# Splitting the left operands of the down product where they are made

## Chip, cores and metric

The kernel runs on one core of a Trainium2 chip. The metric is the device time of one execution in microseconds (us). All data are float32. TensorE (PE) multiplies, VectorE (DVE) and GpSimd (POOL) do elementwise work, ScalarE (ACT) does copies and activation functions, and the queue of SyncE (SP) issues the DMAs.

## What is computed

One block of an encoder for 1024 tokens of width 1024: a SwiGLU layer of half weight, a combined attention of two kinds, a second SwiGLU layer, with an RMSNorm before and after each.

```python
def _rmsnorm(x, g):
    r = lax.rsqrt(jnp.mean(x * x, axis=-1, keepdims=True) + EPS)
    return x * r * g

def _swiglu(x, w_gate, w_up, w_down):            # D_FF = 2816 = 22 * 128
    return (jax.nn.silu(x @ w_gate) * (x @ w_up)) @ w_down

f = _swiglu(_rmsnorm(x, ffn1_pre_g), ffn1_w_gate, ffn1_w_up, ffn1_w_down)
x = x + 0.5 * _rmsnorm(f, ffn1_post_g)
h = _rmsnorm(x, mix_pre_g)
qkv = h @ w_qkv
...
x = x + _rmsnorm(heads @ w_out, mix_post_g)
f = _swiglu(_rmsnorm(x, ffn2_pre_g), ffn2_w_gate, ffn2_w_up, ffn2_w_down)
x = x + 0.5 * _rmsnorm(f, ffn2_post_g)
```

## The kernel before

Every float32 operand of a product is split into two parts of a shorter float type (HI, and LO, the rest), and a product runs as three passes (HI HI, HI LO, LO HI). The function `split` makes the parts: an ACT copy for HI (L118), then a subtraction on DVE or POOL for LO (L119).

Both SwiGLU layers are objects of the class `Ffn`, with the same code. Their products are done in 2 x 2 blocks by a scheme that needs seven products in place of eight (P1 to P7). The gate and up weights are worked through in 22 column blocks i of 128. Blocks 1 to 21 run as items ("G", i, product), each of 12 matmuls of 128 x 512, in the order of `ORDER`: P1, P6, P2, P7, P5, P4, P3 (`LAST` for block 21). P2 adds to the PSUM bank on which P1 stood, after P1 has been copied out to the tile U (`gate_up`, L416). The sums U and C (tiles U2, U3, C21) are formed by DVE; `glu` takes silu on ACT (L449) and multiplies on DVE (L450). Its results are the four left operands of the down product for each pair j of blocks: tiles h of 128 x 512. `feed` prepares weights up to five tiles ahead of their use: for gate/up it splits the loaded weights (tile wgu from rawgu), and POOL forms their sums in place (L215, L216, L225, L227).

Pairs j = 0 to 10 of blocks make up the inner dimension of the down product, with seven products k each; 77 items ("D", k, j), 12 matmuls each. `GROUPS` takes pairs 0 to 4 first, then 5 to 10. After the odd block of a pair, `keep` stores the seven left operands of the pair to DRAM (hd): three as they are, four after an add on DVE, which are queued in `late` and emitted one for each item that follows (`add_late`). `load_left` loads them back (tile h, pool of `HBUFS` = 10), in the order of use, which begins with product 1 of pairs 0 to 4; `AHEAD` = 4 loads come early. `prepare_down` splits both operands of an item, left (h) and right (blocks b11 to b22 of the down weights).

What sets the order is the order of emission; on each engine instructions run in the program's order, and each waits for what it reads or overwrites. SP's queue holds loads and stores in one order as well.

In the first layer, `run` takes `jobs`: the post norms of rows 4 to 7 and parts of the next layer's norm (`stat1`, `post1`, `mix1`, `turn1`) are emitted between the last items of the down phase; what is left stands between the layer and the qkv projection.

Of the kernel before, what the change touches and what calls it, by code (L numbers as in the profile page):

```python
# [36 lines left out]
def tile_macaron_block(ctx, tc, x, f1_pre, f1_post, f1_g, f1_u, f1_d, mix_pre, mix_post, w_qkv,  # L37
# [83 lines left out]
    class Ffn:  # L121
# [6 lines left out]

        ORDER = ("P1", "P6", "P2", "P7", "P5", "P4", "P3")
# [8 lines left out]
        AHEAD = 4  # L138

        def __init__(self, wg, wu, wd, tag, far):  # L140
# [8 lines left out]
            for it in self.items:  # L149
                self.tiles += [it] if it[0] == "G" else [it + (z,) for z in range(2)]  # L150
            self.wanted = [d[1:] for d in downs]
            self.hd = {}
            for key in self.wanted:
                self.hd[key] = dram.tile([128, 512], F32, name=f"hd{tag}" + "_".join(str(z) for z in key))
            self.made = self.used = 0
            self.dw = {}
            self.late, self.late2 = [], []
# [43 lines left out]
        def feed(self):  # L201

            while self.made < len(self.tiles) and self.made - self.used < self.WBUFS:
                it = self.tiles[self.made]
                self.made += 1
                {"G": self.prepare, "D": self.prepare_down}[it[0]](*it[1:])
# [32 lines left out]
        def load_left(self, n):  # L239

            for _ in range(n):
                if self.wanted:
                    key = self.wanted.pop(0)
                    self.A[key] = self.dn.tile([128, 512], F32, name="h")
                    SP.dma_start(self.A[key], self.hd[key])

        def prepare_down(self, k, j, part):

            sub, add, tt = OP.subtract, OP.add, DVE.tensor_tensor
            if part == 0:  # L250
                self.load_left(1)
                self.split_w((j, k, 0), self.A.pop((k, j)), DVE)
                return
# [6 lines left out]
            self.split_w((j, k, 1), (b11, b21, b11, b12, b12, b11, b22)[k], DVE)  # L260
# [73 lines left out]
        def keep(self, j):  # L334

            a11, a21, a12, a22 = [self.H[2 * j + c][b] for c in range(2) for b in range(2)]
            for k, t in ((0, a11), (1, a12), (4, a22)):
                SP.dma_start(self.hd[k, j], t)
            S = {"a11": a11, "a12": a12, "a22": a22, "s1": a21}

            def made(k, o, p, q, op):
                if o not in S:
                    S[o] = self.dn.tile([128, 512], F32, name="h")
                DVE.tensor_tensor(S[o], S[p], S[q], op=op)
                SP.dma_start(self.hd[k, j], S[o])

            for z in ((5, "s1", "s1", "a22", OP.add), (2, "s2", "s1", "a11", OP.subtract),
                      (3, "s3", "a22", "s2", OP.subtract), (6, "s4", "a12", "s2", OP.subtract)):
                self.late.append(lambda z=z: made(*z))

        def down(self, k, js, y, ps, psd, row=None):
# [6 lines left out]
            for i in range(4):  # L358
# [6 lines left out]
                for j in js:  # L365
                    A, B = [self.W[j, k, z].rearrange("p a k f -> p a (k f)") for z in range(2)]
                    for n, (a, b) in enumerate(PASSES):
                        PE.matmul(p, A[:, a, 128 * i:128 * i + 128], B[:, b, :],  # L368
# [10 lines left out]
                elif k == 2:  # L379
                    tt(U[i], U[i], p, op=add)  # L380
                    if g:
                        self.late += [lambda v=v, i=i: tt(v, v, U[i], op=add) for v in (y11, y10)]
                        self.late2.append(lambda v=y01, i=i: tt(v, v, U[i], op=add))
# [18 lines left out]
        def gate_up(self, i, prod, ps, y, psd):  # L402
# [40 lines left out]
            if n == 6 and i % 2 == 1:  # L443
                self.keep(i // 2)
            if n == 6 and i == NF - 1:
                self.U = [U(name).rearrange("p t f -> p (t f)") for name in ("U2", "U2", "C21", "U3")]
# [5 lines left out]
        def run(self, ps, y, psd, jobs, row):  # L452
# [4 lines left out]
            for n, it in enumerate(self.items):  # L457
                if n == at:
                    self.late += self.late2
                    self.add_late(len(self.late) - len(self.late2))  # L460
# [3 lines left out]
                if n < at - 18 or n >= at - 6 or n >= at - 12 and n % 2 == 0:  # L464
# [7 lines left out]
                else:  # L472
                    self.down(it[1], it[2:], y, ps, psd)
                    self.used += 2
# [83 lines left out]
    def post_early(T, g):  # L558
# [6 lines left out]
        DVE.tensor_tensor(yh, yh, g[:, 0:512], op=OP.mult)  # L565
# [87 lines left out]
    def early1():  # L653
        for T in range(4):
            post_early(T, E1["g"])
# [549 lines left out]
```

## Time and profile before

| what | us |
|---|---|
| median of three runs | 2038.09 (2037.31 to 2041.84) |
| profiled execution | 2038.71 |
| its span in the trace | 2036.9 |
| gate/up, first layer, about | 60 to 472 |
| down, first layer, about | 472 to 695 |
| gate/up, second layer, about | 1392 to 1802 |
| down, second layer, about | 1802 to 2025 |

The span is the time from the first to the last instruction in the trace; the profiled execution takes 1.8 us more than it. A duration in a row is that of one instruction or of a run of equal ones. "Idle before" is the time that the engine stood still ahead of an instruction, with the instruction of another engine that ended it. A matmul's end is modelled, so that two may overlap in a row.

### The profile page before, as it was taken

What the parts mean: (1) busy time and instruction counts of PE and PEld (TensorE: products, weight loads), DVE (VectorE), ACT (ScalarE), POOL (GpSimd) and SP (SyncE); (2) the same over time, 40 slices, a digit from 0 to 9 for tenths busy, and PEclk for the clock granted to TensorE, in tenths of its full rate; (3) what the DMA queues carried; (4) which work ended last, traced back from release to release, by engine and by line L of the source; (5) the groups of instructions that cost most, each with busy time, mean ns of one, the idle gap of its engine ahead of it and who ended that gap; (6) DMA issues with size and microseconds to landing.
All of it is one profiled execution on the core that took longest, in us unless ns stands there. A gap on an engine that the chain in (4) does not pass through costs nothing.

```text
span 2036.9 us, 30471 instructions
## 1 busy us (share of the span) xinstructions
PE 1976.9 (97%) x10704; PEld 1675.1 (82%) x10704; DVE 1351.0 (66%) x2435; ACT 1030.5 (51%) x1977; POOL 840.7 (41%) x768
## 2 busy tenths in 40 slices
PE   7999999999999899999999999999999999999996
PEld 6777777778878699998999998887777777788785
DVE  7645554557878838756989888356545455577787
ACT  5433333334445734547999999234333333344444
POOL 4566656560000002124777887315565666600000
PEclk9999999999999899999999999999999999999998
DMA  5232332428534542232050743322223232375343
GB/s 150 74 102 95 113 103 79 130 82 274 182 109 144 183 131 78 78 93 59 1 140 13 205 133 93 104 78 73 94 88 121 86 104 93 109 268 176 120 130 138
DMA packets 212441, 235.62 MB, mean 116 GB/s; under 512 B 22209, under 2 KB 148161, under 8 KB 212161
## 3 DMA queue, kind: packets, MB, share of 16 engines
q1 hardware_dynamic: 212288, 233.69, 36.7%
q8 instruction: 84, 1.38, 0.3%
q14 instruction: 69, 0.56, 0.1%
HBM read 166.01 MB, written 67.63 MB: 115 GB/s over the span
## 4 chain that ended last, share of the span: by engine, by line
PE 70%; POOL 11%; ACT 6%; DVE 5%; issue 4%; DMA 3%; SPq 0%; DVEq 0%; ACTq 0%; POOLq 0%
PE pq L608 10%; PE pd L368 8%; PE pa L294 8%; PE pc L294 6%; PE pd L294 5%; PE pt L935 5%; POOL wgu L119 5%; PE pz L1073 4%; PE pb L294 3%; PE pa L368 3%; ACT wgu L118 3%; PE po L959 3%; PE pb L368 3%; PE pc L368 3%; PE sp L845 3%
## 5 line engine op out<-in xcount | busy, mean ns | idle before, releaser
L119 POOL TENSOR_TENSOR wgu<-rawgu,wgu 128x512 fp32r<-128x512 f32 x216 | 312.9, 1457 | 359.5 <-ACT wgu L118 333.4
L118 ACT ACTIVATE wgu<-rawgu 128x512 fp32r<-128x512 f32 x302 | 181.7, 628 | 377.6 <-POOL rawgu L227 189.6
L294 PE MATMUL pa<-actT,wgu 128*128 128x512 f32 (+1 forms) x1080 | 268.2, 395 | 7.9 <-ACT U L416 7.9
L294 PEld LDWEIGHTS pa<-actT,wgu 128*128 128x128 f32 x1080 | 197.1, 189 | 63.5 <-ACT U L416 20.1
L368 PE MATMUL pd<-wgu 128*128 128x512 f32 x948 | 236.3, 393 | 7.5 <-DVE wgu L119 6.9
L368 PEld LDWEIGHTS pd<-wgu 128*128 128x128 f32 x948 | 178.3, 189 | 49.2 <-DVE wgu L119 10.6
L608 PE MATMUL pq<-wq,actT 128*128 128x256 f32 x1728 | 217.4, 283 | 0.6 <-DVE actT L109 0.6
L608 PEld LDWEIGHTS pq<-wq,actT 128*128 128x128 f32 x1728 | 208.4, 189 | 1.4 <-DVE actT L109 0.9
L118 ACT ACTIVATE wgu<-b 128x512 fp32r<-128x512 f32 x154 | 97.2, 631 | 218.9 <-PE pd L368 209.6
L73 POOL TENSOR_SCALAR gpost<-gpost 128x1024 f32<-128x1024 f32 x2 | 2.6, 1294 | 387.5 <-DVE wgu L119 194.5
L838 POOL TENSOR_SCALAR P<-P,il 128x1024 f32<-128x1024 f32 (+1 forms) x128 | 130.5, 1020 | 66.7 <-DVE il L837 62.7
L119 DVE TENSOR_TENSOR wgu<-b,wgu 128x512 fp32r<-128x512 f32 x154 | 106.1, 689 | 76.5 <-ACT wgu L118 76.4
L450 DVE TENSOR_TENSOR h<-h,C 64x512 f32<-64x512 f32 x42 | 49.6, 1182 | 160.8 <-ACT h L449 160.8
L939 DVE TENSOR_TENSOR PT<-pt,PT 128x512 fp32r<-128x512 f32 (+1 forms) x256 | 146.0, 611 | 2.0 <-ACT PT L938 2.0
L294 PE MATMUL pc<-actT,wgu 128*128 128x512 f32 x552 | 136.5, 395 | 0.0
L294 PE MATMUL pd<-actT,wgu 128*128 128x512 f32 x552 | 136.0, 395 | 0.0
L938 ACT ACTIVATE PT<-pt 128x512 fp32r<-128x512 f32 (+1 forms) x256 | 125.2, 544 | 12.3 <-PE pt L935 8.8
L935 PE MATMUL pt<-identr,P 128*128 128x128 f32 x896 | 124.9, 274 | 2.0 <-ACT vst L773 1.0
L294 PEld LDWEIGHTS pd<-actT,wgu 128*128 128x128 f32 x552 | 103.4, 187 | 25.3
L294 PEld LDWEIGHTS pc<-actT,wgu 128*128 128x128 f32 x552 | 103.4, 188 | 25.3 <-DVE actT L109 0.4
L294 PE MATMUL pb<-tx,wgu 128*128 128x512 f32 x504 | 122.9, 392 | 0.0
L294 PE MATMUL pc<-tx,wgu 128*128 128x512 f32 x504 | 122.4, 392 | 0.0
(204 smaller groups left out, 3978.6 us busy)
## 6 DMA issues: line engine op xcount, KB each, us to landing
hd<-h SPq DMA_DIRECT2D x154, 256.0 KB, 2.8
h<-hd SPq DMA_DIRECT2D x154, 256.0 KB, 2.9
rawgu<-in_ffn_w_gate_dram SPq DMA_DIRECT2D x88, 256.0 KB, 3.0
rawgu<-in_ffn_w_up_dram SPq DMA_DIRECT2D x88, 256.0 KB, 3.5
b<-in_ffn_w_down_dram SPq DMA_DIRECT2D x88, 256.0 KB, 3.6
bkT<-kd SPq DMA_DIRECT2D x32, 320.0 KB, 7.6
rawq<-in_w_qkv_dram SPq DMA_DIRECT2D x16, 512.0 KB, 4.9
bV<-vd SPq DMA_DIRECT2D x8, 640.0 KB, 3.9
```

The lines of the kernel that those rows point to most:

```text
L118: ACT.activation(hi, raw, AF.Copy)
L119: return eng.tensor_tensor(lo, raw, f32(hi), op=OP.subtract).ins
L294: PE.matmul(p[:, c0:c1, :], w[:, a, k, :], self.rhs(name, b, k)[:, c0:c1, :], start=(first and n == 0), stop=(n == 11), skip_group_check=True)
L368: PE.matmul(p, A[:, a, 128 * i:128 * i + 128], B[:, b, :], start=(first and start and j == js[0] and n == 0), stop=(end and j == js[-1] an ...
L608: PE.matmul(p, actT[:, a, k, T, :], WQ[j][:, b, k, :], start=(n == 0), stop=(n == 23))
L838: POOL.tensor_scalar(P[:, 0:w], P[:, 0:w], il, 1.0, op0=OP.mult, op1=OP.mult)
L845: PE.matmul(sp[:, 512 * half:512 * half + 512], col(qT[:, h, :], T), kT[:, a, 512 * half:512 * half + 512], start=(a == 0), stop=(a == 1))
L935: PE.transpose(out=p[:, j, :], in_=col(P, b0 + j), identity=ident)
L938: ACT.activation(hv, p[:, 0:n, :], AF.Copy)
L939: DVE.tensor_tensor(lv, p[:, 0:n, :], f32(hv), op=OP.subtract)
L959: PE.matmul(o, V[:, k, :], pt[:, a, k, :], start=(n == 0), stop=(n == 15))
L1073: PE.matmul(p[:, 512 * dh:512 * dh + 512], actT[:, a, c, T, :], WO[c][:, b, 512 * dh:512 * dh + 512], start=(n == 0), stop=(n == 23))
```

## The change

The left operands are split in gate/up, when they are made. `keep` queues seven jobs for a pair. Each does its add (if it has one), splits the operand by an ACT copy and a DVE subtraction into a row of y (which is free at that time; y holds the layer's rows before and after), and stores both halves with one DMA of 512 KB. `load_left` loads two halves of 256 KB, and `prepare_down` splits the right operand alone, so that five prepared tiles are five items. `AHEAD` is 2; at the last gate/up item seven late jobs and three loads are emitted, then one load for each item. The norms of rows 6 and 7 move into `run`.

```diff
-        AHEAD = 4
+        AHEAD = 2
...
-                self.tiles += [it] if it[0] == "G" else [it + (z,) for z in range(2)]
+                self.tiles.append(it)
...
-                self.hd[key] = dram.tile([128, 512], F32, name=f"hd{tag}" + "_".join(str(z) for z in key))
+                self.hd[key] = dram.tile([128, 1024], F32, name=f"hd{tag}" + "_".join(str(z) for z in key))
...
+                if it[0] == "D" and not self.dw:
+                    break
...
-                    self.A[key] = self.dn.tile([128, 512], F32, name="h")
-                    SP.dma_start(self.A[key], self.hd[key])
-
-        def prepare_down(self, k, j, part):
+                    self.A[key] = [self.dn.tile([128, 512], FR, name="h") for _ in range(2)]
+                    for z, t in enumerate(self.A[key]):
+                        SP.dma_start(f32(t), self.hd[key][:, 512 * z:512 * z + 512])
+
+        def prepare_down(self, k, j):
...
-            if part == 0:
-                self.load_left(1)
-                self.split_w((j, k, 0), self.A.pop((k, j)), DVE)
-                return
...
-        def keep(self, j):
+        def keep(self, j, y):
 
             a11, a21, a12, a22 = [self.H[2 * j + c][b] for c in range(2) for b in range(2)]
-            for k, t in ((0, a11), (1, a12), (4, a22)):
-                SP.dma_start(self.hd[k, j], t)
-            S = {"a11": a11, "a12": a12, "a22": a22, "s1": a21}
-
-            def made(k, o, p, q, op):
-                if o not in S:
-                    S[o] = self.dn.tile([128, 512], F32, name="h")
-                DVE.tensor_tensor(S[o], S[p], S[q], op=op)
-                SP.dma_start(self.hd[k, j], S[o])
-
-            for z in ((5, "s1", "s1", "a22", OP.add), (2, "s2", "s1", "a11", OP.subtract),
-                      (3, "s3", "a22", "s2", OP.subtract), (6, "s4", "a12", "s2", OP.subtract)):
-                self.late.append(lambda z=z: made(*z))
+            S = {0: a11, 1: a12, 4: a22, 5: a21, 3: y[:, 7, 0:512], 6: y[:, 7, 512:1024]}
+
+            def made(n, k, p=None, q=None, op=None):
+                if op:
+                    if k == 2:
+                        S[k] = self.dn.tile([128, 512], F32, name="h")
+                    DVE.tensor_tensor(S[k], S[p], S[q], op=op)
+                st = y[:, n, :]
+                hi, lo = [st[:, 512 * z:512 * z + 512].bitcast(FR) for z in range(2)]
+                split(hi, lo, S[k], DVE)
+                SP.dma_start(self.hd[k, j], st)
+
+            for n, z in enumerate(((0,), (1,), (4,), (5, 5, 4, OP.add), (2, 5, 0, OP.subtract),
+                                   (3, 4, 2, OP.subtract), (6, 1, 2, OP.subtract))):
+                self.late.append(lambda n=n, z=z: made(n, *z))
...
-                self.keep(i // 2)
+                self.keep(i // 2, y)
             if n == 6 and i == NF - 1:
+                self.add_late(7)
+                self.load_left(self.HBUFS // 2 - self.AHEAD)
...
-                if n < at - 18 or n >= at - 6 or n >= at - 12 and n % 2 == 0:
+                if not at - 18 <= n < at - 12:
                     self.add_late(1)
...
-                    self.used += 2
+                    self.used += 1
+                    self.load_left(1)
...
-            post_scale(Ts, post_rstd(Ts), E1["g"], [E1["xr", T] for T in Ts], lambda T: x1d[T], 512)
+            post_scale(Ts, post_rstd(Ts), E1["g"], [E1["xr", T] for T in Ts], lambda T: x1d[T])
...
-           {0: [begin1, lambda: stat1((4, 5)), lambda: post1(4)], 1: [lambda: post1(5)], 3: [lambda: mix1((4, 5))],
-            5: [early1], 6: [first_q], 7: [lambda: stat1((6, 7)), lambda: post1(6)], 8: [lambda: post1(7)],
-            9: [lambda: turn1(4), lambda: turn1(5)]}, row1)
+           {0: [begin1, lambda: stat1((4, 5)), lambda: post1(4)], 1: [lambda: post1(5)], 2: [lambda: stat1((6, 7))],
+            3: [lambda: mix1((4, 5)), lambda: post1(6)], 4: [lambda: post1(7)], 5: [early1], 6: [first_q],
+            7: [lambda: mix1((6, 7))], 8: [lambda: turn1(4)], 9: [lambda: turn1(5), lambda: turn1(6)]}, row1)
...
-    mix1((6, 7))
+    turn1(7)
     mix1((0, 1))
-    turn1(6)
     first(0, 4)
-    turn1(7)
     first(0, 5)
```

The first place is ACT's queue around the end of a block of gate/up. Before, the silu of C is followed at once by the copy L416 of the next block's P1 (pa) to U:

```order
L449 ACTIVATE C21_2192<-U3_2251 64x512
L118 ACTIVATE wgu_2295<-rawgu_2091 128x2x4x64
L449 ACTIVATE h_2229<-C21_2192 64x512
L118 ACTIVATE wgu_2316<-rawgu_2091 128x2x4x64
L449 ACTIVATE C21_2192<-U2_2191 64x512
L416 ACTIVATE U2_2334<-pa_2321 128x512
L118 ACTIVATE wgu_2340<-rawgu_2194 128x2x4x64
```

After the change, at the end of the odd block of a pair (L452 is the silu, L417 the copy of P1; y<-h is the ACT half of a left operand's split):

```order
L452 ACTIVATE C21_2554<-U3_2613 64x512
L118 ACTIVATE wgu_2657<-rawgu_2439 128x2x4x64
L452 ACTIVATE h_2591<-C21_2554 64x512
L118 ACTIVATE y_154<-h_2591 128x512
L118 ACTIVATE wgu_2675<-rawgu_2439 128x2x4x64
L452 ACTIVATE C21_2554<-U2_2553 64x512
L118 ACTIVATE y_154<-h_2633 128x512
L417 ACTIVATE U2_2694<-pa_2681 128x512
```

Two copies y<-h have moved in, one behind the silu of h and one ahead of the copy L417. At the end of an even block the first of them stands there alone.

The second place is DVE's queue at the same end of a block, after the change (L453 is the product in `glu`, L434 the update of U by P3; y<-h,y is the subtraction of a split):

```order
L431 TENSOR_TENSOR C_2997<-U_2996,pc 128x512
L453 TENSOR_TENSOR h<-h,C_2997 64x512
L119 TENSOR_TENSOR y<-h,y 128x512
L434 TENSOR_TENSOR U_2996<-U_2996,pd 128x512
L119 TENSOR_TENSOR wgu<-rawgu,wgu 128x2x4x64
L453 TENSOR_TENSOR h<-C_2997,U_2996 64x512
```

The subtraction stands between the product in `glu` and the update of U; before, the update followed the product directly.

The third place is SP's queue at the start of the first layer's down phase. In hd11_2 the first 1 is the layer, the second the product, and 2 is the pair. Before, the loads of the first items are followed by weight blocks:

```order
L245 DMA h_3703<-hd11_1_75 128x512
L245 DMA h_3705<-hd11_2_76 128x512
L245 DMA h_3707<-hd11_3_77 128x512
L245 DMA h_3709<-hd11_4_78 128x512
L237 DMA b21_3725<-in_ffn1_w_down_dram 128x512
L237 DMA b21_3727<-in_ffn1_w_down_dram 128x512
L237 DMA b21_3729<-in_ffn1_w_down_dram 128x512
L237 DMA b21_3731<-in_ffn1_w_down_dram 128x512
L237 DMA b22_3733<-in_ffn1_w_down_dram 128x512
L245 DMA h_3758<-hd10_0_79 128x512
L237 DMA b22_3778<-in_ffn1_w_down_dram 128x512
L338 DMA hd11_10_144<-h_3755 128x512
```

After the change, the stores of pair 10's left operands (L347) stand among the loads:

```order
L347 DMA hd11_10_144<-y_154 128x1024
L347 DMA hd14_10_132<-y_154 128x1024
L249 DMA h_3959<-hd11_2_76 128x512
L347 DMA hd15_10_138<-y_154 128x1024
L347 DMA hd12_10_120<-y_154 128x1024
L347 DMA hd13_10_126<-y_154 128x1024
L347 DMA hd16_10_150<-y_154 128x1024
L249 DMA h_3960<-hd11_2_76 128x512
L249 DMA h_3963<-hd11_3_77 128x512
L249 DMA h_3964<-hd11_3_77 128x512
L249 DMA h_3967<-hd11_4_78 128x512
```

The reload of hd11_2 has moved behind two stores of pair 10, and its second half behind all of them but the first operand's.

## Rows read from the trace of the kernel before

**Rows 1.** Page, part 1: busy us (share of the span) and instructions of each engine.

```profile
PE 1976.9 (97%) x10704; PEld 1675.1 (82%) x10704; DVE 1351.0 (66%) x2435; ACT 1030.5 (51%) x1977; POOL 840.7 (41%) x768
```

**Rows 2.** Waits of PE over the run: us in total, times, longest us.

```profile
PE pa L294 <- ACT U L416: 7.9, 18, 2.2
```

**Rows 3.** Chain of waits, window 395 to 425: start us, us, what.

```profile
414.67 0.63 ACT h L449
...
416.60 0.70 DVE U L433
...
417.38 0.63 ACT C L449
...
418.04 0.61 ACT U L416
...
421.75 2.75 PE pc L294 x12
```

**Rows 4.** Timeline of PE, three starts of P2: start us, us, instruction, idle before.

```profile
379.24 0.73 PE L294 MATMUL pa<-actT,wgu 128*128 128x512 f32 x2 [0.23 <-ACT U L416]
...
398.79 0.68 PE L294 MATMUL pa<-actT,wgu 128*128 128x512 f32 x2
...
418.69 0.73 PE L294 MATMUL pa<-actT,wgu 128*128 128x512 f32 x2 [0.23 <-ACT U L416]
```

**Rows 5.** Timeline of ACT, 396 to 418.

```profile
398.09 0.60 ACT L416 ACTIVATE U<-pa 128x512 f32<-128x512 f32 x1
...
401.85 0.59 ACT L449 ACTIVATE h<-pa 64x512 f32<-64x512 f32 x1 [2.12 <-PE pa L294]
...
407.53 1.16 ACT L118 ACTIVATE wgu<-rawgu 128x512 fp32r<-128x512 f32 x2 [4.43 <-POOL rawgu L216]
```

**Rows 6.** Groups of instructions by form, window 100 to 440.

```profile
L118 ACT ACTIVATE wgu<-rawgu 128x512 fp32r<-128x512 f32 x122 | 73.1, 628 | 151.9 <-POOL rawgu L227 79.4 <-POOL rawgu L216 71.7
...
L344 DVE TENSOR_TENSOR h<-h 128x512 f32<-128x512 f32 x34 | 32.2, 947 | 0.9
...
L450 DVE TENSOR_TENSOR h<-C,U 64x512 f32<-64x512 f32 x35 | 24.4, 698 | 22.3 <-ACT C L449 22.3
L450 DVE TENSOR_TENSOR h<-h,C 64x512 f32<-64x512 f32 x18 | 22.2, 1235 | 76.6 <-ACT h L449 76.6
...
L433 DVE TENSOR_TENSOR U<-U,pd 128x512 f32<-128x512 f32 x18 | 12.4, 687 | 0.6
```

**Rows 7.** Timeline of DVE, end of gate/up of the first FFN.

```profile
473.37 0.68 DVE L433 TENSOR_TENSOR U<-U,pd 128x512 f32<-128x512 f32 x1
473.96 0.69 DVE L119 TENSOR_TENSOR wgu<-h,wgu 128x512 fp32r<-128x512 f32 x1
```

**Rows 8.** DMA issues: out<-in, count, KB each, median us to landing.

```profile
h<-hd SPq DMA_DIRECT2D x154, 256.0 KB, 2.9
```

**Rows 9.** Timeline of PE, start of the down phase and waits with ends.

```profile
471.64 0.63 PE L368 MATMUL pa<-wgu 128*128 128x512 f32 x2
...
665.14 3.70 PE L368 MATMUL pd<-wgu 128*128 128x512 f32 x9 [2.92 <-DVE wgu L119]
...
690.03 0.73 PE L368 MATMUL pa<-wgu 128*128 128x512 f32 x2 [2.12 <-DVE wgu L119]
...
704.61 0.69 PE L107 MATMUL pd<-identr,y 128*128 128x128 f32 x2 [4.08 <-ACT y L647]
```

**Rows 10.** Windows of core 0: busy us (count) by engine, granted clock, DMA share, GB/s.

```profile
472.00:695.00 223.00, 215.28 (x943) 175.47 (x942) 181.99 (x304) 113.17 (x207) 1.06 (x1) 0.99 0.52 167
695.00:729.00 34.00, 29.33 (x216) 28.50 (x216) 22.70 (x62) 25.68 (x53) 0.00 (x0) 0.85 0.59 185
666.00:668.00 2.00, 2.00 (x6) 1.55 (x5) 2.00 (x9) 1.69 (x5) 0.00 (x0) 0.50 0.87 260
...
690.00:692.00 2.00, 1.97 (x9) 1.63 (x10) 2.00 (x4) 0.00 (x0) 0.00 (x0) 1.00 0.92 248
704.00:713.00 9.00, 7.80 (x34) 7.18 (x35) 5.77 (x12) 9.00 (x17) 0.00 (x0) 0.50 0.80 269
```

More of the change, by code (lines that the diff above doesn't have):

```diff
@@ L153, in __init__ @@
             for key in self.wanted:
-                self.hd[key] = dram.tile([128, 512], F32, name=f"hd{tag}" + "_".join(str(z) for z in key))
+                self.hd[key] = dram.tile([128, 1024], F32, name=f"hd{tag}" + "_".join(str(z) for z in key))
             self.made = self.used = 0
             self.dw = {}
-            self.late, self.late2 = [], []
+            self.late = []
         def open_raw(self):
@@ L259, in prepare_down @@
             b11, b12, b21, b22 = [self.B[j, name] for name in self.BLOCKS]
-            self.split_w((j, k, 1), (b11, b21, b11, b12, b12, b11, b22)[k], DVE)
+            self.split_w((j, k), (b11, b21, b11, b12, b12, b11, b22)[k], DVE)
             def diff(j):
@@ L365, in down @@
                 for j in js:
-                    A, B = [self.W[j, k, z].rearrange("p a k f -> p a (k f)") for z in range(2)]
+                    A, B = self.A[k, j], self.W[j, k].rearrange("p a k f -> p a (k f)")
                     for n, (a, b) in enumerate(PASSES):
-                        PE.matmul(p, A[:, a, 128 * i:128 * i + 128], B[:, b, :],
+                        PE.matmul(p, A[a][:, 128 * i:128 * i + 128], B[:, b, :],
                                   start=(first and start and j == js[0] and n == 0),
@@ L381, in down @@
                     if g:
-                        self.late += [lambda v=v, i=i: tt(v, v, U[i], op=add) for v in (y11, y10)]
-                        self.late2.append(lambda v=y01, i=i: tt(v, v, U[i], op=add))
+                        self.late += [lambda v=v, i=i: tt(v, v, U[i], op=add) for v in (y11, y10, y01)]
                 elif g:
@@ L458, in run @@
                 if n == at:
-                    self.late += self.late2
-                    self.add_late(len(self.late) - len(self.late2))
+                    self.add_late(len(self.late))
                     for name in ("b12", "b11"):
@@ L556, in tile_macaron_block, with post_early @@
     SS = {}
-    def post_early(T, g):
+    def post_early(T, g=None):
         if T % 2 == 0:
@@ L564, in post_early @@
                        accum_out=SS[T // 2][:, 0, T % 2:T % 2 + 1])
-        DVE.tensor_tensor(yh, yh, g[:, 0:512], op=OP.mult)
+        if g is not None:
+            DVE.tensor_tensor(yh, yh, g[:, 0:512], op=OP.mult)
     def post_late(T):
@@ L654, in early1 @@
         for T in range(4):
-            post_early(T, E1["g"])
+            post_early(T)
     def turn1(T):
```

## The prediction

> **What bounds the kernel now.** I read the busy table first: TensorE (PE) is busy 97% of the span, VectorE (DVE) 66%, ScalarE (ACT) 51% [rows 1]. So a change can gain only where PE waits, and can lose wherever something on another engine gets late. The list of PE's waits is short. Most of it lies in the down phases, behind DVE's splits, and one wait ahead of the qkv projection. Then there are 18 waits for the copy of product P1 out of bank a (L416), 7.9 us together [rows 2]. They are in the gate/up phases, are small, and are what matters here, so I read the chain of waits over one block of gate/up [rows 3]. It is a closed loop. P2 accumulates on the bank that P1 used, so it cannot start before L416 has copied P1 out. From P2's matmuls (398.79 [rows 4]) the chain goes to the silu of h (401.85, after an idle 2.12 that PE ends [rows 5]), which stands ahead of a weight split in ACT's queue. POOL's split and its sums for the next block (L215, L216) follow, then ACT's next copies (407.53, after an idle 4.43 that POOL ends [rows 5]), POOL's next work, and then the tail in [rows 3]: the silu of h (414.67), DVE's U update L433 (416.60), the silu of C (417.38), the U copy L416 (418.04), and P2 of the next block (418.69 [rows 4]). P2 starts at 379.24, 398.79 and 418.69, at two of them after an idle 0.23 [rows 4]. At 398.79 the copy (start 398.09, 0.60) had ended 0.1 us earlier [rows 5]. So there is at most 0.1 us to spare. One item is 2.75 us of matmuls [rows 3], and a pair of blocks takes 39.45 us. Whatever is put into the loop's serial part lengthens the block.
>
> **What the change puts there.** Per pair of blocks seven splits (an ACT copy into y, a DVE subtraction) move from the down phase into gate/up. Their places are seen in the two lists of ACT and the one of DVE. After an even block, the copy y<-h stands behind the silu of h, and DVE's subtraction of it stands ahead of the U update. The copy needs the h that DVE's L453 has just finished, so copy and subtraction run one after the other before the U update may start: 0.63 + 0.69 us by the nearest rows (the ACT copy of 128x512, 628 ns; DVE's 128x512 ops that have POOL idle beside them, 687 ns) [rows 6]: **1.32**. After an odd block the same stands there, and a second copy stands between the silu of C and the U copy. It splits the h that L453 has to finish after that silu (0.69), then the copy itself takes 0.63: another 1.32, **2.64** in all. A pair of blocks: 3.96.
>
> The other four splits of a pair stand right behind the U copy, while P2 runs, and behind the first weight split after P2. There ACT is idle 2.12 us before 401.85 and 4.43 before 407.53 [rows 5], so their copies cost nothing directly. Without that idle each would cost its 0.63.
>
> **Contention.** DVE's h<-h,C takes 1235 ns with a POOL op beside it, the same shape h<-C,U takes 698 with POOL idle; the add L344 takes 947 on average [rows 6]. All seven new subtractions read two SBUF operands, and some five of them lie beside the POOL part of the loop. If each stretches POOL by as much as L344 is stretched (0.26 over 687), a pair costs 1.3 more, with rounding up to 1.6. The least is 0. The stretch of before that has such adds beside POOL (398.79 to 418.69, 19.90) is 0.35 longer than its neighbour (19.55) [rows 4]; I take 0.4, near that row. The Trainium skill's page "GPSIMD Engine Reference", section "8. Key points", says that GpSimd shares its SBUF interfaces with VectorE and contends with VectorE instructions that have two SBUF inputs, and so speaks against the change. The 1235 beside 698 agrees.
>
> **Sum of gate/up.** Pairs run 0 to 10; the last one's late work falls into the down phase, and the first blocks are still filling, so nine full pairs (the 18 waits of [rows 2] are nine for each FFN). 9 x 3.96 = 35.6, with contention 9 x 4.36 = 39.2; times two FFNs, since both run the same code: 71 to 78. At the high bound (1.6 of contention, ten pairs) it is 111. I take **+78**. PE should then wait 0.23 + 1.32 + 0.4, some 1.9 us, before the P2 that follows an even block, and 2.5 (2.64 less the 0.1) before the one that follows an odd block.
>
> **Start of the down phase.** SP's list shows the reload of the third item (hd11_2: product 1, pair 2) behind two stores of the last late splits, and its second half behind the last store. Those stores wait for DVE. From the U update (473.37 in before) DVE has 20 operations in order up to the last subtraction. Such ops start 0.59 apart [rows 7], with their waits some 0.61, so the last ends near 485.6, the store and the second half are issued at 486.3, and a reload takes 2.9 from issue to landing [rows 8], so it lands at 489 to 490.5 with two halves and stores in the queue. The first half (after 9 or 10 operations, 479.5) lands at 482 to 483. PE begins the down phase at 471.64 [rows 9] and wants the item at 471.64 + 2 x 2.75 = 477.1. It waits 5 to 6 us for the first half, works 8 of 12 matmuls (1.8), and waits 4.5 to 6 for the other: 9.5 to 11.5. After idle stretches of 2.92 and 4.08 [rows 9] the granted clock stands at 0.50, the lower level, for some us (666 to 668, 704 to 713 [rows 10]). In before, idle time plus this is the price; I add 2 for it. **13.5 per FFN, 27 in all** (bounds 18 and 32).
>
> **What comes back.** A down item no longer splits its left operand: 0.63 on ACT and 0.69 on DVE less, 77 times per FFN. DVE is busy 182 of 223 us there [rows 10], and is what PE waits for. The look-ahead of the right operands also doubles in items (five tiles are five items, before two and a half). FFN1's down phase takes 223.0 with PE busy 215.3: 7.7 us idle, and some 2 to 3 us of half clock after 665.14. FFN2 runs the same code. I take 9 and 10 of some 10 in each. Ahead of qkv, 695 to 729 has 4.7 us idle and a half clock over 704 to 713 [rows 10], after the 4.08 us wait for L647 [rows 9]. The norms of rows 6 and 7 (the L647 that PE waits for) now run inside the down phase, where ACT and DVE have the room that the splits left. I take 5 (bounds 2 and 6). post_scale over whole rows adds about 0.6 for each of the four rows at the end, beside qkv matmuls, where PE does not wait; uncovered it would be 2.4 in all. **-24.** Stores and loads of hd double, from 256 KB to 512 KB an item. At a DMA share of 0.52 in the down phase [rows 10] the second reload fits, and its stores are gone from there.
>
> **Sum.** 2038.71 (the profiled run, 0.6 above the median of the three; its span is 2036.9) + 78 + 27 - 24 = 2119.7, so **2120**. The likeliest case alone reaches from 2098 (no contention 71, start 18, gains 30) to 2160 (gate/up 111, start 32, gains 22).
>
> **Rivals.**
> The clock falls too. A wait of 2.5 us before every second P2 lies between 2.12 (690.03), after which the clock stays at 1.00, and 2.92 (665.14), after which it is 0.50 [rows 9, 10]. The lower level covers the 2 us of that row, from 666, and what lies on both sides of it; I take 3.8 us from 665.14 on, in which half the rate costs 1.9, all of it in P2, which is part of the loop. 18 such waits are +34: 2154. For it: 2.5 is in the open middle, and a POOL op stretched by 0.4 makes it 2.9. Against: PE is busy without a break for the 16 us before. Chance 0.24.
> The splits are hidden. If the queues run on so that copy and subtraction fit into idle time (between ACT's silu of h, 414.67 to 415.30, and its silu of C at 417.38 lies only one copy of 0.63 [rows 3, 6]), gate/up costs nothing and the sum is 2038.7 + 27 - 24 = 2041, within 0.2%. Against: that idle time is itself the wait on L433, which comes later by the same amount. Chance 0.10.
> Faster. The splits are hidden and the start wait is short as well: if the adds and subtractions on DVE before the last store take under 12 us, or the reloads are taken around them, each FFN's start costs 9 or less, below its 12 of gain: 2038.7 + 18 - 26 = 2031. It needs the DVE string at the start of the down phase to be the only place that decides, and that string cut to half of its 20 operations. The freed 0.69 of DVE per item speaks for it. Chance 0.10.
>
> **Numbers.** Likeliest 0.56. A difference of 0.2% (4 us) is about what a measurement of this kernel tells from no change. Faster 0.10, the same 0.05, slower 0.85: the likeliest case and the clock rival are slower, 0.80, and the hidden-splits case (2041, bounds 2028 to 2049) gives 0.05 to the same and 0.05 to slower, and the last rival its 0.10 to faster. For 8 in 10 the range covers the likeliest case and the clock rival but for their ends: 2075 to 2165.
>
> **What would show it.** In the changed profile: some 18 waits on the U copy (now L417) in each FFN, of 1.9 and 2.5 us in turn, and stretches of 22.2 and 21.6 us in place of 19.55 and 19.90; waits at the third item of each down phase of 4 to 6 us, twice; no waits on DVE's wgu later in it; no 4 us ahead of qkv. It is wrong if gate/up keeps its 39.45 us a pair, or if the waits before P2 are longer than these insertions because a POOL op is stretched more than 0.4.

## The result and the profile after

The changed kernel takes 2143.1 us (median of four; 2140.8 to 2144.7) beside 2038.6 of the kernel before: a ratio of 1.051 (95% interval 1.049 to 1.053), 104.5 us slower. The profiled span is 2139.0, 102.1 more than before. The forecast was 2120, in a range of 2075 to 2165.

The two traces were laid side by side by PE's first instruction of each stage:

| stretch, by PE's timeline | before | after | difference |
|---|---|---|---|
| start to the first down item | 471.6 | 523.8 | +52.2 |
| first down phase, to the first qkv matmul | 223.1 | 226.9 | +3.8 |
| qkv, to the first transpose behind it (L771, now L773) | 144.8 | 136.7 | -8.0 |
| attention and out projection, to the second gate/up | 515.5 | 517.4 | +1.9 |
| second gate/up, to the first down item | 447.2 | 497.5 | +50.3 |
| second down phase, to the end of its matmuls | 222.2 | 224.6 | +2.4 |

So 102.5 us are lost in the two gate/up phases, and the rest comes to nothing. The busy table of the changed kernel, which answers to [rows 1]:

```profile
PE 1987.4 (93%) x10704; PEld 1677.0 (78%) x10704; DVE 1438.1 (67%) x2431; ACT 1035.4 (48%) x1977; POOL 854.3 (40%) x768
```

PE is busy 93% in place of 97%. Its waits, in the list that answers to [rows 2], name the places:

```profile
PE pa L294 <- ACT U L417: 47.9, 22, 2.3
PE pc L294 <- DVE U L422: 39.7, 20, 2.0
PE pa L370 <- DMA h<-hd: 19.1, 4, 6.0
PE pd L294 <- DVE U L425: 9.4, 18, 0.6
```

The 18 waits for the copy of P1 were 7.9 us; now there are 22, and they take 47.9. New are two groups that the prediction does not have, for the U updates L422 and L425 on DVE: 49.1 us. PE's timeline over one pair of blocks shows them in order (P2, P4, P3, the next P2, and the P2 after that; compare [rows 4]):

```profile
398.78 3.07 PE L294 MATMUL pa<-actT,wgu 128*128 128x512 f32 x12 [2.29 <-ACT U L417]
...
409.31 3.05 PE L294 MATMUL pc<-actT,wgu 128*128 128x512 f32 x12 [1.98 <-DVE U L422]
412.90 3.04 PE L294 MATMUL pd<-actT,wgu 128*128 128x512 f32 x12 [0.54 <-DVE U L425]
...
421.34 2.98 PE L294 MATMUL pa<-actT,wgu 128*128 128x512 f32 x12
...
443.26 2.13 PE L294 MATMUL pa<-actT,wgu 128*128 128x512 f32 x8 [2.29 <-ACT U L417]
```

A pair takes 443.26 - 398.78 = 44.48 us in place of 39.45: the even block 22.56 (19.90 before), the odd one 21.92 (19.55 before). One wait of 2.29 stands at the odd block's end; 1.98 and 0.54 stand inside the even block; the P2 that follows the even block waits for nothing. The chain of waits into the odd block's end is the one that the prediction drew, with the two copies y<-h in it (compare [rows 3]):

```profile
437.40 1.24 DVE h L453
438.66 0.63 ACT y L118
...
439.94 0.69 DVE U L434
440.71 0.64 ACT C L452
441.37 0.70 DVE h L453
442.09 0.63 ACT y L118
442.72 0.48 ACT U L417
```

From the product in `glu` (437.40) to P2 (443.26) are 5.86 us. Before, the product started at 415.33, and to P2 at 418.69 were 3.36:

```profile
415.33 1.24 DVE L450 TENSOR_TENSOR h<-h,C 64x512 f32<-64x512 f32 x1 [4.47 <-ACT h L449]
```

That is 2.50 more now. The other place is seen in DVE's timeline inside the even block, ahead of L422:

```profile
403.72 1.33 DVE L343 TENSOR_TENSOR y<-h 128x512 f32<-128x512 f32 x1
404.98 1.78 DVE L119 TENSOR_TENSOR y<-h,y 128x512 fp32r<-128x512 f32 x1
406.68 1.76 DVE L343 TENSOR_TENSOR y<-h 128x512 f32<-128x512 f32 x1
408.48 0.69 DVE L422 TENSOR_TENSOR U<-U,pc 128x512 f32<-128x512 f32 x1
```

and in that of POOL at the same time:

```profile
404.47 1.74 POOL L218 TENSOR_TENSOR rawgu<-rawgu 128x512 f32<-128x512 f32 x1
406.29 1.61 POOL L219 TENSOR_TENSOR rawgu<-rawgu 128x512 f32<-128x512 f32 x1
```

Adds and subtractions that take 0.69 alone take 1.33 to 1.78 here, one after the other, and L422 stands behind them. It reads bank c, and P4 cannot start on that bank before L422 has ended (409.17). POOL's sums take 1.74 and 1.61 in place of 1.29.

PE's timeline at the start of the first down phase (compare [rows 9]) and two windows of it (compare [rows 10]):

```profile
523.83 0.86 PE L370 MATMUL pa<-wgu,h 128*128 128x512 f32 x3
...
535.51 1.19 PE L370 MATMUL pa<-wgu,h 128*128 128x512 f32 x2 [6.00 <-DMA h<-hd]
...
542.15 0.80 PE L370 MATMUL pa<-wgu,h 128*128 128x512 f32 x1 [2.89 <-DMA h<-hd]
```

```profile
523.83:750.00 226.17, 217.28 (x950) 178.66 (x949) 143.43 (x240) 85.13 (x151) 1.60 (x1) 0.97 0.78 267
535.00:539.00 4.00, 3.49 (x8) 2.48 (x8) 3.97 (x8) 0.70 (x2) 0.00 (x0) 0.50 1.02 405
```

The third item waits for its two halves, 6.00 and 2.89 us, and the clock then stands at 0.50.

### The profile page after: what moved, and what is told of

Same layout as the page of the kernel before. It is cut to its first block, busy times and chain, and to the rows that moved or that the text cites. A ratio compares the mean times of both kernels' runs of the same rounds, so it can differ in the third digit from the quotient of the medians.

```text
span 2139.0 us, 30720 instructions
## 1 busy us (share of the span) xinstructions
PE 1987.4 (93%) x10704; PEld 1677.0 (78%) x10704; DVE 1438.1 (67%) x2431; ACT 1035.4 (48%) x1977; POOL 854.3 (40%) x768
## 3 DMA queue, kind: packets, MB, share of 16 engines
q8 instruction: 85, 1.39, 0.3%
## 4 chain that ended last, share of the span: by engine, by line
PE 60%; DVE 15%; POOL 9%; ACT 7%; issue 5%; DMA 3%; SPq 0%; DVEq 0%; POOLq 0%; ACTq 0%
PE pd L370 9%; PE pq L612 9%; PE pa L294 6%; PE pt L937 5%; POOL wgu L119 4%; PE pz L1075 4%; PE pd L294 3%; PE pb L294 3%; ACT wgu L118 3%; PE pa L370 3%; PE pb L370 3%; PE po L961 3%; PE pc L370 3%; DVE y L119 3%; DVE y L343 3%
## 5 line engine op out<-in xcount | busy, mean ns | idle before, releaser
L119 POOL TENSOR_TENSOR wgu<-rawgu,wgu 128x512 fp32r<-128x512 f32 x216 | 304.9, 1420 | 449.9 <-ACT wgu L118 435.4
L118 ACT ACTIVATE wgu<-rawgu 128x512 fp32r<-128x512 f32 x302 | 186.4, 625 | 271.9 <-POOL rawgu L230 127.6
L294 PE MATMUL pa<-actT,wgu 128*128 128x512 f32 (+1 forms) x1080 | 269.1, 397 | 48.8 <-ACT U L417 47.9
L370 PE MATMUL pd<-wgu,h 128*128 128x512 f32 x948 | 232.6, 391 | 0.0
L370 PEld LDWEIGHTS pd<-wgu,h 128*128 128x128 f32 x948 | 178.8, 189 | 37.8 <-DVE U L434 0.5
L294 PE MATMUL pc<-actT,wgu 128*128 128x512 f32 x552 | 141.0, 405 | 39.7 <-DVE U L422 39.7
L119 DVE TENSOR_TENSOR y<-h,y 128x512 fp32r<-128x512 f32 x110 | 111.2, 1012 | 44.6 <-ACT y L118 44.6
L294 PEld LDWEIGHTS pd<-actT,wgu 128*128 128x128 f32 x552 | 102.1, 188 | 40.3 <-issue 16.7
```

What stands on the lines that cost most here:

```text
L118: ACT.activation(hi, raw, AF.Copy)
L119: return eng.tensor_tensor(lo, raw, f32(hi), op=OP.subtract).ins
L294: PE.matmul(p[:, c0:c1, :], w[:, a, k, :], self.rhs(name, b, k)[:, c0:c1, :], start=(first and n == 0), stop=(n == 11), skip_group_check=True)
L370: PE.matmul(p, A[a][:, 128 * i:128 * i + 128], B[:, b, :], start=(first and start and j == js[0] and n == 0), stop=(end and j == js[-1] an ...
```

## The experiments

All times are medians of four to ten runs, but for five kernels that ran once: no subtractions, half of each store, held splits, one SBUF input, and POOL for the last pair alone. The kernel before took 2038.6 to 2041.0 beside them.

**The norms alone.** The kernel before with the later part of the diff: the jobs of `f1.run`, `post_early` without the gain, whole rows in `post_scale`.

> The kernel before with the reordered norms of the first layer alone; the left operands are split in the down phase as before. If the norms are what empties the wait ahead of the qkv projection (the changed kernel gained 8.0 us from the first qkv matmul to the first transpose behind it): that stretch is 6 to 8 us shorter here too, the 4.08 us wait for L647 is gone, and the whole is 4 to 8 us faster than before (about 2032). Rival: the norms only fit because the down phase has lost 77 splits; here DVE and ACT are still full, the down phase grows by what the transition loses, and the whole is within 3 us of before.

2031.6 us, ratio 0.9955 (0.9941 to 0.9968). From the first qkv matmul to the first transpose behind it the trace takes 135.9 us (144.8 before), and of the wait of 4.08 us on the norm's ACT copy 0.8 is left. The first down phase, to the first qkv matmul, takes 224.0 (223.1 before), so it does not take up what the transition loses. The reordered norms gain 9 us by themselves, a little more than expected, without the room that the splits leave, and the rival falls. This is the fastest kernel of the study.

**No subtractions.** In `made`:

```diff
-                split(hi, lo, S[k], DVE)
-                SP.dma_start(self.hd[k, j], st)
+                ACT.activation(hi, S[k], AF.Copy)
+                SP.dma_start(self.hd[k, j][:, 0:512], st[:, 0:512])
```

> The changed kernel without the seven DVE subtractions of a pair in gate/up; the ACT copies and the adds remain. Left out is the LO part of the left operands (the HI half is stored, half as much, and loaded twice). Theory of the prediction (insertions at the ends of blocks alone, pair 3.96): an odd end keeps two copies and the wait for the product in glu, some 1.9 us before P2, an even end 0.5; a pair is near 42. What the trace of the changed kernel suggests (DVE's string of adds and subtractions ahead of the U updates L422 and L425, stretched by POOL, holds PE in the even block for 2.5 us): these waits go to under 0.4 us, those before P2 stay at 1 to 2, a pair takes 41 to 41.5, the whole about 2080. If the DMA traffic of the larger stores were the cause: the waits on L422 stay in proportion to bytes, and no single engine's wait vanishes.

2079.1 us. A pair takes 41.98 (P2 at 398.83 and 440.81). PE's waits:

```profile
PE pa L294 <- ACT U L417: 41.4, 40, 2.2
...
PE pc L294 <- DVE U L422: 6.0, 20, 0.3
```

The 20 waits on L422 are down to 0.3 each and those on L425 are gone. 64 us went with the seven subtractions; 52 of them lie in the two gate/up phases, 2.6 a pair, and most of the rest in the down phases. The string on DVE is a cause of its own. With those waits gone, PE waits at the end of the even blocks too (0.46 at 440.81, beside 1.55 at the end of the odd one): 40 waits on the copy of P1 in place of 22.

**Half of each store, all the work.** This is the control for the run above:

```diff
-                SP.dma_start(self.hd[k, j], st)
+                SP.dma_start(self.hd[k, j][:, 0:512], st[:, 0:512])
```

> The changed kernel with all its ACT and DVE work, but half of each store: 256 KB, HI alone; both reloads read HI (the LO part is left out of the product). It is the control for the run without subtractions, which also stored half. If the engines' queues are what costs: a pair still takes 44 to 44.6 us, and the whole is within 6 us of the changed kernel (2137 to 2146). If the doubled stores delay the weight loads or the reloads: gate/up shrinks by 1 us or more a pair, and the whole is below 2125.

2144.9 us, with the same waits as in the changed kernel:

```profile
PE pa L294 <- ACT U L417: 48.0, 22, 2.4
PE pc L294 <- DVE U L422: 39.8, 20, 2.0
```

The two gate/up phases are together 6 us longer than in the changed kernel, because here seven products behind such waits run at the lower level of PE's clock (P2 then takes 4.61 us in place of 3.07), where one does in the changed kernel. That is some 9 us by their durations. So the doubled stores cost at most some 3 us in gate/up.

**All splits held off the ends of the blocks.** `gate_up` keeps the copy of P1 and the U update by P3, and the jobs are traced behind them:

```diff
+                    if self.late and not (it[1] % 2 and it[2] == "P3"):
+                        with tc.issue_after(self.copied), tc.issue_after(self.updated):
+                            self.add_late(2)
```

> The changed kernel with all seven late splits of a pair held behind the copy of P1 of the next even block (ACT) and behind the U update (DVE), two for each item, so that none stands at a block's end. Theory of the prediction: the waits before P2 (2.29 us) go, and a pair takes 39.5 to 40.5, the whole about 2060. String on DVE: the waits before P2 go as well, but seven splits, not four, now stand ahead of L422 and L425 in the even block, so PE's waits there grow from 2.5 to 4.5 us or more, a pair takes 43.5 to 46, and the whole is 2120 to 2175.

2157.0 us. The waits on the copy of P1 fall to 3.8 us in all, as both expected. The waits on L422 grow:

```profile
PE pc L294 <- DVE U L422: 84.0, 20, 6.3
```

P4 behind one of them, in PE's timeline:

```profile
411.45 4.38 PE L294 MATMUL pc<-actT,wgu 128*128 128x512 f32 x12 [4.05 <-DVE U L422]
```

That is 4.2 us each, and a pair takes 44.60. The theory of the prediction, which knew only the ends, would have had 2060. Most of what the splits cost at the ends they cost again ahead of L422, but not all: the waits of a pair are 4.2 us beside 4.8 in the changed kernel. What comes on top is the clock: behind 17 of the 20 waits P4 runs at the lower level and takes 4.31 to 5.46 us in place of 3.05, some 30 us in all. Without that, by these durations, the kernel would have taken some 2127 us, less than the changed one.

**The splits placed.** All seven stand where DVE and ACT are idle in before: on ACT between the silu of P5 and the weight split that waits for POOL, on DVE between the C sum of P4 and the product in `glu`. The adds stand about where they were before.

```diff
-                tt(s["c21"], s["u2"], p, op=add)
+                at = tt(s["c21"], s["u2"], p, op=add).ins
...
+                if i > 1:
+                    with tc.issue_after(self.silu5), tc.issue_after(at):
+                        self.add_late(4 if i % 2 == 0 and i < NF - 2 else 7)
...
+                self.load_left(self.HBUFS // 2 - self.AHEAD)
                 self.add_late(7)
-                self.load_left(self.HBUFS // 2 - self.AHEAD)
```

> The changed kernel with the splits of a pair placed in the idle time of DVE and ACT ahead of the silu of h: behind the C sum of P4 on DVE and behind the silu of P5 on ACT, four in the even block and three in the odd one; the four adds of a pair stand where the kernel before had them; the reloads of items 3 to 5 stand ahead of the last pair's stores. If the place in the queues is what costs (strings ahead of L422 and L425 and of the U copy): a pair takes 39.4 to 40.0 us, no wait of PE in gate/up is above 0.6, and the whole is 2030 to 2046, with the wait on h<-hd of some 17 us still in it, at the sixth item of each down phase. If DVE's use of SBUF beside POOL is what costs wherever it stands: the sums L228 and L230 of POOL, now beside the splits, go from 1.29 to 1.5 us or more each, a pair takes 41 or more, and the whole is 2060 or more.

2068.9 us: 74 us less than the changed kernel, but inside what was expected of contention, and a pair takes 41.14. The groups by form in gate/up (compare [rows 6]):

```profile
L119 DVE TENSOR_TENSOR y<-h,y 128x512 fp32r<-128x512 f32 x42 | 47.9, 1186 | 0.0
...
L230 POOL TENSOR_TENSOR rawgu<-rawgu 128x512 f32<-128x512 f32 x17 | 27.6, 1622 | 1.3
L228 POOL TENSOR_TENSOR rawgu<-rawgu 128x512 f32<-128x512 f32 x16 | 26.4, 1651 | 1.3
```

In the kernel before, L228 is L225 and L230 is L227:

```profile
L227 POOL TENSOR_TENSOR rawgu<-rawgu 128x512 f32<-128x512 f32 x17 | 22.0, 1293 | 1.3
```

POOL's L228 and L230 now take 1.65 and 1.62 in place of 1.29. They are links of the loop (the weight split ahead of the silu of h waits for L230), so the 0.7 us go into each block. The subtractions wait for nothing (idle 0.0). The splits have no queue in front of PE's bank here, and still cost 33 us in the two gate/up phases over the kernel with the norms alone (488.7 to the first down item beside 471.3, and 463.4 beside 447.6 for the second). PE's waits:

```profile
PE pa L294 <- ACT U L419: 34.2, 38, 2.2
...
PE pd L372 <- ACT wgu L118: 8.3, 2, 4.9
PE pa L372 <- ACT y L118: 3.8, 1, 3.8
PE pa L372 <- DMA h<-hd: 3.7, 1, 3.7
```

**One SBUF input.** The kernel with placed splits, its instructions in the same order in gate/up, with this in `made`:

```diff
-                split(hi, lo, S[k], DVE)
+                ACT.activation(hi, S[k], AF.Copy)
+                DVE.tensor_scalar(lo, S[k], 0.5, 1.0, op0=OP.mult, op1=OP.mult)
```

> The kernel with placed splits, in the same order of instructions, with the seven subtractions of a pair replaced by a DVE operation of the same size and form of output that reads h alone (0.25 h in place of LO; the LO part is left out). If two SBUF inputs beside POOL are what stretches: POOL's L228 and L230 (1.65 and 1.62 us there) fall to 1.29 to 1.35, the waits on the U copy from 34 us to under 12, a pair from 41 or more to about 39.5, and the whole from 2069 to 2035 to 2042. If any DVE operation on SBUF beside POOL does it, one input or two: L228 and L230 stay above 1.5 and the whole stays above 2055.

2041.1 us. A pair takes 39.81 (P2 at 383.69 and 423.50); the groups by form and the waits:

```profile
L348 DVE TENSOR_SCALAR y<-h 128x512 fp32r<-128x512 f32 x43 | 37.2, 911 | 0.0
...
L230 POOL TENSOR_TENSOR rawgu<-rawgu 128x512 f32<-128x512 f32 x18 | 24.4, 1355 | 1.4
...
L228 POOL TENSOR_TENSOR rawgu<-rawgu 128x512 f32<-128x512 f32 x17 | 23.5, 1385 | 1.3
```

```profile
PE pa L294 <- ACT U L420: 10.2, 18, 2.2
```

POOL's sums are back at 1.36 to 1.39, and the waits on the copy of P1 at 18 and 10.2 us. So a two-input operation of DVE beside POOL, in place of a one-input one, was worth 28 us of the whole; the stores are the same in both kernels and are not the cause. One thing is not kept apart: the one-input operation is also shorter (0.42 us alone, at the start of the down phase, where POOL is idle). How much of the 28 us is the second input and how much the length is not shown. Beside POOL the one-input operation is stretched too, to 0.91 on average where it reads h and to 1.52 for the two operands that lie in y.

**Earlier reloads.** The changed kernel with

```diff
-                    if k == 2:
-                        S[k] = self.dn.tile([128, 512], F32, name="h")
+                    if k == 2:
+                        S[k] = S[5]
...
+                self.load_left(self.HBUFS // 2 - self.AHEAD)
                 self.add_late(7)
-                self.load_left(self.HBUFS // 2 - self.AHEAD)
```

> The changed kernel with the reloads of items 3 to 5 of the down phase emitted ahead of the last pair's late splits (and the sum of product 2 written over that of product 5, so that a slot is free). If the reload waits in SP's queue behind stores that wait for DVE: the four waits on h<-hd (19.1 us) go to under 3 us in all, the clock stays at 1.00 after them, and the whole is 22 to 32 us faster than the changed kernel, 2111 to 2121. If it is the load on the DMA engines (share 0.97 to 1.05 there) that makes the reloads late: the waits stay at half or more, and the gain is under 12 us.

2175.9 us, ratio to before 1.066: slower than the changed kernel, which neither side expected. PE's waits:

```profile
PE pa L294 <- ACT U L417: 93.4, 40, 2.7
PE pd L370 <- DMA h<-hd: 15.7, 2, 7.9
...
PE pa L370 <- DMA h<-hd: 2.1, 2, 1.2
```

It was not one edit. The sum of product 2 written over that of product 5 has to wait for that one's split, and the scheduler placed the pair's work anew: PE now waits at the end of every block, 40 times. These waits are in sum about as long as all of PE's waits in gate/up in the changed kernel (100 us beside 97). What makes the kernel slower is the clock: behind 26 of the 40 waits P2 runs at the lower level and takes 4.25 to 4.62 us in place of 3.06 (lines in the last section), some 39 us in all, and the two gate/up phases are 39 us longer. In the down phases, which the experiment was for, the wait at the third item is down to 1.2 us, and a wait of 7.9 us stands at the sixth, whose reload is the first one behind the stores. So SP's order decides which item waits. That the lateness of the stores sets how long is argued, not shown.

**More reloads ahead, and POOL for the last pair.** Three variations of the kernel with placed splits: `load_left(self.HBUFS // 2 - self.AHEAD + 3)` ahead of the last pair's jobs; the last pair's subtractions on POOL (`split(hi, lo, S[k], POOL if j == self.PAIRS - 1 else DVE)`); and both.

> As the kernel with placed splits, with three more reloads (items 6 to 8 of the down phase) in SP's queue ahead of the last pair's stores. If only SP's order holds the reloads: the waits on h<-hd go from some 17 us to under 5, the clock is 1.00 in the first 40 us of both down phases, and the whole is 18 to 28 us below the kernel with placed splits (about 2015), faster than both kernels. If the stores are what must be done first (y is wanted again at the end of item 5), PE waits for y or for the splits instead, and the gain is under 8 us.

2063.0 us, 5.9 less than without. The rival held: the waits on the reloads are down to 3.0 us, and PE waits for ACT in the same stretch.

```profile
PE pd L372 <- ACT wgu L118: 5.3, 2, 3.0
...
PE pa L372 <- DMA h<-hd: 3.0, 1, 3.0
```

> As the kernel with placed splits, with the last pair's seven subtractions on POOL, which has no other work there. If DVE's string of 20 operations times the stores: the string is 13 long, the last store is issued some 3 to 4 us earlier, the wait at the sixth item falls from 7.9 to about 4, and the whole is 6 to 10 us less. If POOL (1.29 each, and stretched by DVE beside it) is no faster: the waits are as before or longer by up to 3 us each.

2071.6 us; the waits on reloads are 21.4 us in four waits, where the kernel without has 15.8 us for reloads and ACT together. POOL is no faster than DVE's string, as the second case expected.

> The last two together: three more reloads ahead of the stores, and the last pair's subtractions on POOL. If SP's order is the whole of the wait, this gives the time of the former alone, within 3 us; if the stores' own lateness still counts, 4 to 8 us less than that.

2067.3 us, 4.3 above the reloads alone, which neither case expected. The two edits don't add up, and the start of the down phase was not freed of its price.

**The left split on POOL, in the down phase.** The kernel with the reordered norms alone, and

```diff
-                self.split_w((j, k, 0), self.A.pop((k, j)), DVE)
+                self.split_w((j, k, 0), self.A.pop((k, j)), POOL if (k + j) % 3 == 0 else DVE)
```

> The kernel before with the reordered norms, and with the left split's subtraction on POOL in every third item of the down phases, where POOL has no other work. If DVE's load is what PE waits for there (its waits on wgu are 10.9 us in all with the reordered norms): these fall by half or more, and the whole is 4 to 9 us below the kernel with reordered norms alone (about 2025). If POOL and DVE stretch each other as in gate/up: DVE's subtractions beside POOL go from 0.69 to 1 us or more, the waits stay or grow, and the whole is the same or up to 15 us slower.

2045.7 us, ratio 1.0028 (1.0018 to 1.0037), so 14 us slower than the norms alone. The groups by form in the first down phase, and PE's waits:

```profile
L119 POOL TENSOR_TENSOR wgu<-h,wgu 128x512 fp32r<-128x512 f32 x24 | 38.1, 1590 | 166.4 <-ACT wgu L118 145.5 <-DVE y L386 13.7 <-DMA b<-in_ffn_w_down_dram 7.2
```

```profile
PE pd L368 <- DVE wgu L119: 8.9, 8, 3.6
...
PE pa L368 <- DVE wgu L119: 7.5, 5, 4.0
PE pd L368 <- POOL wgu L119: 2.8, 2, 1.4
```

A subtraction takes 1.59 on POOL, and PE's waits on splits grow from 10.9 us (7.1 and 3.8) to 19.2. The rival was right about the time. DVE's own subtractions stay at 0.68 (of h) and 0.74 (of b) on average in this phase, but one group of its sums of b goes from 0.68 to 1.08, and the subtraction on POOL is itself 0.9 longer than on DVE. Which of these PE's waits come from was not tried.

## Why the prediction was right, and where it was off

The direction was right, and so was the mechanism for about half of the price: work was put into the serial part of a loop that had 0.1 us to spare, in both layers alike. The other half came in a place that the prediction had put at nothing. The sum was 23 us short, and all of it in one term, gate/up: +78 forecast, +102.5 measured. A pair was to cost 4.36 us and cost 5.03. That the two are so near is partly luck, since a price at the even block's end that did not come stands against one inside the even block that was not forecast. Point by point:

- **The odd block's end.** 2.64 forecast for the insertions and a wait of 2.5; measured 2.50 and 2.29. Right.
- **The other four splits.** That "their copies cost nothing directly" is the step that failed. It looked at ACT's idle time alone. The subtractions and adds of the same jobs stand on DVE, two of the four subtractions ahead of L422, on whose bank P4 waits, and two ahead of L425, on whose bank P3 waits; and beside POOL each of them takes 1.33 to 1.78. The measured waits are 1.98 and 0.54 a pair. Without the subtractions they go to 0.3; with three more splits there they grow to 4.2.
- **The even block's end.** 1.32 and a wait of 1.9 were forecast, none came. The insertion is in the chain, but PE was already late by the waits inside the block. Two waits in one loop don't add up: without the subtractions, when the waits inside are gone, a wait of 0.46 does come at this end.
- **Contention.** 0.4 us a pair was taken, out of 0 to 1.6, by what the old adds cost. Measured with the splits placed, it is near the high end: gate/up is 25.7 us longer with two SBUF inputs than with one, 1.3 us for each of 20 pairs. The Trainium skill's "GPSIMD Engine Reference", section "8. Key points", which names VectorE instructions with two SBUF inputs, deserved this end. The traces agree with it, 1.65 beside 1.39 for POOL's L228. In the changed kernel itself this part is not separated from the waits above. One reading was wrong: of the 35 h<-C,U in [rows 6], taken as 698 "with POOL idle", 17 lie beside a POOL operation and take 0.70 all the same. There it is POOL's side that is longer (two weight splits in 3.00 us from 408.24 on, where a single one at 414.72 takes 1.30).
- **The number of pairs.** Ten, not nine: 20 waits on L422 in the list, and 10 x 5.03 = 50.3 is the second layer's whole loss.
- **Start of the down phase.** 9.5 to 11.5 us of waits and 2 of low clock were forecast for each layer, 13.5. Measured in the first: 8.9 of waits, and the lower level from 535.5 to some 547 us, in which 8.8 us of work cost 4.4 more, 13.3. The place is right; the sum agrees by two misses that cancel, the wait for the second half (2.9, 4.5 to 6 forecast) and the clock. In the second layer it is some 14 (10.2 of waits).
- **What comes back.** -24 forecast. No wait on DVE's splits is left in the down phases. With the start's price taken off, the first regains some 9.5 us and the second some 12, beside 9 and 10, and qkv gains 8.0 beside 5. The down phases and qkv come to -1.8 in all, where +3 was forecast. The experiment with the norms alone shows that the 8.0 come from them and not from the splits. The 1.9 us of attention were not followed; 1.0 of them is there with the norms alone too.
- **The clock rival** did not come true in the changed kernel, where the clock stays at 1.00 after waits of 2.29; a single P4 of the second layer, after a wait of 1.98, ran at the lower level (4.59 us). It did in the experiments: 26 blocks with earlier reloads, 17 with held splits, seven with half of each store, at some 1.4 to 1.8 us each on average, where the rival had 1.9. **The hidden splits** and **the faster case** fall with the waits above. The run with one SBUF input, 2041, stands where the hidden-splits case put its sum; this suggests that those cases needed a split that neither queues ahead of PE's bank nor meets POOL.

One sentence ahead of the prediction is too simple: the order on an engine is not that of emission alone. A scheduler places what is ready; the first split of a pair stands at the end of the even block, a whole block ahead of where `keep` is called.

So of the 102.5 us in gate/up, 69 are given back by placing the work elsewhere on ACT and DVE, 25.7 lie between placed splits of two inputs and of one, and some 7.5 were not divided further. Most of the 25.7 is seen in POOL's sums: L228 and L230 are together 0.53 us shorter in each of some 40 blocks, 21 us. The first part holds what POOL stretches in the strings ahead of L422 and L425, so the two parts are not fully apart. In the down phases the new start costs some 6 us more than comes back, and the reordered norms give back the 8.0 ahead of the attention. The norms alone are the part that helps.

## What to carry to other kernels

Before work is moved into a phase where an engine is "40% idle", follow the loop that paces the phase and ask of every engine that the work touches, not only of the first, which instruction stands behind it and who waits for that one. An idle stretch on DVE is worth less than it looks while POOL works in SBUF: price it with the row of the same form that overlaps POOL, not with the one that does not. And test the parts of a bundled change one at a time: the part that gained here would have been thrown away with the part that lost. Where a variation comes out slower, look at how long PE's products take as well as at its waits: in two of the variations here the clock, and not the waits, made the difference.

## What the runs showed of the hardware that was not expected

The stretch on both sides was larger than the one row in before suggested. DVE's add y<-h of 128x512 takes 688 ns on average in the kernel with earlier reloads, where it stands clear of POOL, 1550 in the changed kernel and 1804 without the subtractions; POOL's sums take 1.29 alone and up to 1.74 in the changed kernel.

PE's clock does not follow the length of the last wait alone. In the kernel with earlier reloads a wait of 2.70 is followed by full speed, the next one of 2.29 by the lower level, in which P2 takes 4.61 us in place of 3.06. PE's timeline and the windows behind these two waits:

```profile
392.23 3.06 PE L294 MATMUL pa<-actT,wgu 128*128 128x512 f32 x12 [2.70 <-ACT U L417]
...
414.24 4.61 PE L294 MATMUL pa<-actT,wgu 128*128 128x512 f32 x12 [2.29 <-ACT U L417]
```

```profile
392.00:396.00 4.00, 3.77 (x16) 3.09 (x17) 2.32 (x4) 1.86 (x5) 1.29 (x1) 1.00 0.61 176
414.00:418.00 4.00, 3.76 (x10) 2.94 (x11) 3.17 (x5) 1.74 (x4) 1.28 (x1) 0.57 0.85 300
```

In the changed kernel the same 2.29 us leave the clock at 1.00. The kernel with half of each store has both: after a wait of 2.30 P2 takes 4.61 us at 399.82 and 3.07 at 445.84. The kernel with held splits shows 0.63 over 410 to 414, after a wait of 4.05. What tells these cases apart was not tried.
